# Measured times in a list schedule, and operand copies moved to GpSimd

## The chip, the cores and the metric

The kernel runs on one core of a Trainium2 chip. The metric is the device time of one execution in microseconds (us); the runs shown are summed up by their median. TensorE (PE in the profile; PEld is its weight load) multiplies matrices, ScalarE (ACT), VectorE (DVE) and GpSimd (POOL) work on elements, and SyncE (SP) issues most of the DMAs.

## What is computed

Two layers over 256 tokens of width 1024, all in float32. Each layer is a SwiGLU block of hidden width 2816, a token mixer, and a second SwiGLU block, with an RMSNorm ahead of and behind each:

```python
for layer in range(DEPTH):                       # DEPTH = 2
    x = x + 0.5 * rmsnorm(swiglu(rmsnorm(x, g[0]), ...), g[1])
    x = x + rmsnorm(token_mixer(rmsnorm(x, g[2]), w_in, w_out, ...), g[3])
    x = x + 0.5 * rmsnorm(swiglu(rmsnorm(x, g[4]), ...), g[5])
```

The mixer projects to queries, keys and values and runs 16 heads of three kinds side by side: 6 dilated softmax heads ("dil"), 4 differential heads ("diff", the difference of two softmaxes, with queries and keys of width 32) and 6 stick-breaking heads ("stick"). Their outputs are joined and multiplied by `w_out`.

## The kernel before, in words

Each float32 operand of a large product is split into a high part that TensorE multiplies at full speed (type fp32r) and the rest, and a product is three matmuls: high by high, high by low, low by high (`mm3`; every matmul is issued in `mm`, line 403). A weight tile of 128 x 1024 is loaded into one of 5 "raw" buffers, ScalarE writes its high part (line 306) and VectorE the rest (line 309) into one of 10 "ring" buffers.

The program is not written in its running order. `op(engine, us, fn, after, bufs)` notes each step with an estimate of its time. `Program.run` then plays the program through: TensorE's steps get due times in the order in which they were noted, the steps of the other engines get theirs backward from the steps that need them, and whenever an engine is free in this play the most urgent step is issued whose inputs are ready and whose buffers are free. That fixes the order of instructions on each engine. On the chip each engine goes through its list in that order and waits where an input is late. The estimates come from `act_us(n, psum)` and `dve_us(n)` (lines 240 to 245) or stand as figures at the `op`. A hop between engines counts as 0.2 us.

In `mixer` the eight pairs of heads (two heads of one kind, or for diff two heads with two scores each) are taken in the order diff, stick, dil, stick, diff, stick, dil, dil. `qk(i)` projects queries and keys of pair i: two weight tiles, 24 matmuls each, into a PSUM tile. Then operands for the scores are made from it:

- diff (lines 782 to 800): each of the four 32-row blocks gets a tile of its own in which the high part stands twice and the low part twice. ScalarE writes both high copies (line 790, two instructions), VectorE the low part (794) and its copy (795).
- stick and dil (lines 802 to 820): one of the two operands, the "moving" one, is needed with both halves of the partitions exchanged as well. ScalarE writes each half twice (line 806, four instructions; two for the other operand), VectorE the low parts (810), and GpSimd copies the low parts of the moving operand into the other half (814).

`pair(i)` then computes the scores (`scores`, lines 839 to 868: matmuls, VectorE's `least` at 859, ScalarE's `expo` at 863), normalises, transposes, and multiplies with the values; for stick it runs the softplus chain (940 to 951). `stage` interleaves qk(i) with the steps of pairs i-1 and i-2. The products with `w_out` (`out_`, 6 matmuls for a step) and the residual of the first 128 tokens, and then those of the second, close the mixer.

Of the kernel before, what the change touches and what calls it, by code (L numbers as in the profile page):

```python
# [8 lines left out]
F32 = mybir.dt.float32  # L9
F32R = mybir.dt.float32r  # L10
BF16 = mybir.dt.bfloat16
AF = mybir.ActivationFunctionType
# [112 lines left out]
class Program:  # L125
# [7 lines left out]
    def op(self, eng, dur, fn, after=(), bufs=(), spare=None, lag=None):  # L133
        o = Op()
        o.eng, o.dur, o.fn, o.after, o.bufs = eng, dur, fn, [a for a in after if a is not None], list(bufs)
        o.spare, o.lag, o.idx = spare or {}, lag, len(self.ops)
        for b in o.bufs:
            b.left += 1
        self.ops.append(o)
        return o  # L140
# [97 lines left out]


def act_us(n, psum, extra=0):  # L240
    return (0.05 if psum else 0.092) + 0.000833 * n + 0.093 * extra


def dve_us(n):
    return 0.068 + 0.00104 * n


def trunk(tc, x, norm_gains, w_gate, w_up, w_down, w_in, w_out, dlam, subln, consts, out):
    nc = tc.nc
# [6 lines left out]
    op = G.op  # L256
# [16 lines left out]
    QB = tuple(slice(32 * m, 32 * (m + 1)) for m in range(4))  # L273
    HB = (slice(0, 64), slice(64, 128))
# [464 lines left out]
    def mixer(l, xt, turn1, g, nxt, o_cst, o_misc):  # L739
# [17 lines left out]
        tab = [None]  # L757
        qk_, mixed, stages = {}, {}, []

        def qk(i):  # L760

            kind, n = PAIRS[i]
            sc = {"dil": -0.125, "stick": 0.125, "diff": -(32 ** -0.5)}[kind]
            moving = 0 if kind == "stick" else 1
            r = {}
            for part in range(2):  # L770
                h = half_chunk(wi, QK_OFF[kind][part] + 128 * n)
                p = Buf(PS)
                scale = sc if part == 0 else 1.0

                o = None
                for ks in steps(STEPS_Q):
                    def pe(h=h, p=p, ks=ks):
                        w = [t.rearrange("p (k c) -> p k c", k=8) for t in h.ring.t]
                        for k in ks:
                            mm3(p.t[:, :256], w[0][:, k, :], w[1][:, k, :], xt.hi(k, slice(0, 256)), xt.lo(k, slice(0, 256)), k == 0, k == KC - 1)  # L780

                    o = op("PE", 0.327 * len(ks), pe, [o] + sum(xt.done, []) + h.ready, [p, xt.b, h.ring])
                if kind == "diff":
                    for m in range(4):
                        b = Buf(QS, F32R)
                        two = m ^ (2 if part == 0 else 1)

                        def fhi(p=p, b=b, m=m, two=two, scale=scale):
                            for e in (m, two):
                                nc.scalar.activation(b.t[QB[e], :], p.t[QB[m], :256], AF.Copy, scale=scale)  # L790

                        def flo(p=p, b=b, m=m, two=two, scale=scale):
                            e, f = [e for e in range(4) if e not in (m, two)]
                            nc.vector.scalar_tensor_tensor(b.t[QB[e], :], p.t[QB[m], :256], scale, b.t[QB[m], :].bitcast(F32), OP.mult, OP.subtract)  # L794
                            nc.vector.tensor_copy(b.t[QB[f], :], b.t[QB[e], :].bitcast(F32))  # L795

                        o1 = op("ACT", act_us(256, True) * 2, fhi, [o], [p, b])
                        r[part, m] = (b, op("DVE", dve_us(256) + 0.2, flo, [o1], [p, b]))
                    continue
                bs = [Buf(QS, F32R) for _ in range(2)]  # L800
                lo = bs if part != moving else [Buf(QS, F32R) for _ in range(2)]

                def fhi(p=p, bs=bs, scale=scale, both=part == moving):
                    for b in range(2):
                        for e in range(2 if both else 1):
                            nc.scalar.activation(bs[b].t[HB[b ^ e], :], p.t[HB[b], :256], AF.Copy, scale=scale)  # L806

                def flo(p=p, bs=bs, lo=lo, scale=scale, other=part != moving):
                    for b in range(2):
                        nc.vector.scalar_tensor_tensor(lo[b].t[HB[b ^ other], :], p.t[HB[b], :256], scale, bs[b].t[HB[b], :].bitcast(F32), OP.mult, OP.subtract)  # L810

                def fcopy(lo=lo):
                    for b in range(2):
                        nc.gpsimd.tensor_copy(lo[b].t[HB[b ^ 1], :], lo[b].t[HB[b], :].bitcast(F32))

                o1 = op("ACT", act_us(256, True) * (4 if part == moving else 2), fhi, [o], [p] + bs)
                o2 = op("DVE", dve_us(256) * 2, flo, [o1], [p] + bs + (lo if part == moving else []))
                if part == moving:
                    o2 = op("POOL", 0.9, fcopy, [o2], lo)
                r["m" if part == moving else "s"] = bs  # L820
                if part == moving:
                    r["l"] = lo
                r.setdefault("o", []).extend([o1, o2])
            qk_[i] = r
# [13 lines left out]
        def scores(i, r0, n, h, den, d0):  # L838

            qk = qk_[i]  # L840
            p, sn, mn, e = Buf(PS), Buf(SN), Buf(SM), Buf(ES)
            o = C_BIAS + 256 * h
            if n == 32:
                (q, oq), (k, ok) = qk[0, r0 // 32], qk[1, r0 // 32]
                bufs, after, us = [q, k], [oq, ok], 0.22

                def pe():
                    mm(p.t[:, 0:256], q.t[:, B], k.t, True)
                    mm(p.t[:, 256:384], q.t[:, A], k.t[:, A], False, True)
            else:  # L850
                b = r0 // 64
                bufs, after, us = [qk["s"][b], qk["m"][b], qk["l"][b]], qk["o"], 0.40

                def pe():
                    products(p, i, b, ((SEG[0], B, slice(0, 256)), (SEG[1], A, A)))

            def least():
                for a, bs in ((0, slice(o, o + 256)), (1, slice(o + 128, o + 256))):
                    nc.vector.tensor_tensor_reduce(sn.t[:, SEG[a]], p.t[:, SEG[a]], cst[:, bs], 1.0, 3.0e38, OP.add, OP.min, mn.t[:, a:a + 1])  # L859

            def expo():
                for a in range(2):
                    nc.scalar.activation(e.t[:, SEG[a]], sn.t[:, SEG[a]], AF.Exp, bias=mn.t[:, a:a + 1], scale=-1.0, accum_out=den.t[:, d0 + a:d0 + a + 1])  # L863

            o1 = op("PE", us, pe, after, bufs + [p], spare={PS: 2})
            o2 = op("DVE", 0.56, least, [o1, o_cst], [p, sn, mn])
            o3 = op("ACT", 0.88, expo, [o2, tab[0]], [sn, mn, e, den])
            return e, o3

        def transposed(e, oe, c_eng):  # L870
# [18 lines left out]
        def pair(i):  # L889

            kind, n = PAIRS[i]
            c = CHUNK0[kind] + n
            pt = [None, None]
            if kind == "dil":
                es = []
                for b in range(2):
                    den, r = Buf(SM), Buf(SM)
                    e, o = scores(i, 64 * b, 64, 2 * n + b, den, 0)

                    def norm(e=e, den=den, r=r):  # L900
                        nc.vector.reciprocal(r.t[:, 0:2], den.t[:, 0:2])
                        for a, s in enumerate(SEG):
                            nc.vector.tensor_scalar(e.t[:, s], e.t[:, s], r.t[:, a:a + 1], None, OP.mult)

                    es.append((e, op("DVE", 0.67, norm, [o], [e, den, r])))
                yield
                for b in range(2):
                    pt[b] = transposed(*es[b], b)
# [1 line left out]
            elif kind == "diff":  # L910
                es = []
                for b in range(2):
                    den, r = Buf(SM), Buf(SM)
                    (e1, o1), (e2, o2) = (scores(i, 64 * b + 32 * a, 32, N_DIL + 2 * n + b, den, 2 * a) for a in range(2))

                    def comb(e1=e1, e2=e2, den=den, r=r):
                        nc.vector.reciprocal(r.t, den.t)
                        nc.vector.tensor_scalar(r.t[:, 2:4], r.t[:, 2:4], nlam[:, l:l + 1], None, OP.mult)
                        for a, s in enumerate(SEG):
                            nc.vector.tensor_scalar(e2.t[:, s], e2.t[:, s], r.t[:, 2 + a:3 + a], None, OP.mult)  # L920
                        for a, s in enumerate(SEG):
                            nc.vector.scalar_tensor_tensor(e1.t[:, s], e1.t[:, s], r.t[:, a:a + 1], e2.t[:, s], OP.mult, OP.subtract)

                    es.append((e1, op("DVE", 1.6, comb, [o1, o2] + o_misc, [e1, e2, den, r])))
                yield
                for b in range(2):
                    pt[b] = transposed(*es[b], b)
# [1 line left out]
            else:  # L929
                qk = qk_[i]  # L930
                zs = []
                for b in range(2):
# [14 lines left out]
                    def fhi(az=az, sh=sh):  # L947
                        nc.scalar.activation(sh.t[:, :384], az.t, AF.Copy)
# [24 lines left out]
            p = Buf(PS)  # L973
# [201 lines left out]
```

## Time and profile before

| what | us |
|---|---|
| median of 3 runs | 991.08 (990.92 to 991.38) |
| the profiled execution | 991.41 |
| its span, first to last instruction | 989.6 |
| TensorE busy in it | 973.5 |
| VectorE busy | 634.3 |
| ScalarE busy | 595.4 |
| GpSimd busy | 29.5 |

A view by stretches gives for each stretch how long each engine was busy, how many instructions started, and the clock granted to TensorE (1.00 is 2.4 GHz, 0.50 is 1.2 GHz). A view of waits gives for an engine and line what the instruction waited for. A timeline gives instructions in order of time, neighbours of one kind merged (x24), with the idle time before in brackets. "L403" is line 403 of the kernel before.

### The profile page before, as it was taken

The page shows a single profiled execution, that of the slowest core. Times are in us where ns is not written, and L with a number is a line of the kernel's source. Part 1 is how long each engine was busy: PE and PEld are TensorE (multiplying, and loading weights), DVE is VectorE, ACT ScalarE, POOL GpSimd, SP SyncE. Part 2 cuts the span into 40 slices and gives each one's busy share as a digit, 9 for nine tenths or more (in the row PEclk, how much of TensorE's full clock was granted, in tenths as well). Part 3 has the DMA queues.
Part 4 walks back from the last instruction along what each step waited for, and adds up shares of the span by engine and source line. Part 5 has one row for each costly group of instructions (what it writes and reads, how often), then busy time and mean ns, then how long its engine had stood idle before and what let it go on. Part 6 is the DMA issues. An engine that isn't in the chain of part 4 may idle for free.

```text
span 989.6 us, 17271 instructions
## 1 busy us (share of the span) xinstructions
PE 973.5 (98%) x6664; PEld 883.9 (89%) x6664; DVE 634.3 (64%) x1161; ACT 595.4 (60%) x1205; POOL 29.5 (3%) x62
## 2 busy tenths in 40 slices
PE   8999999999999999999999999999999999999997
PEld 6999999888988899999889999998888889999996
DVE  6765544778898656455686555459698876646433
ACT  7754444769997555444665444347899776444442
POOL 0000000000000000000010000001010000000000
PEclk9999999999999999999999999999999999999999
DMA  8986664684336766664577666557732557666531
GB/s 270 325 282 198 189 181 144 200 242 114 126 91 207 255 193 189 197 188 149 173 226 241 194 191 193 169 153 238 213 102 84 167 174 240 189 197 189 165 107 42
DMA packets 147316, 182.79 MB, mean 185 GB/s; under 512 B 6177, under 2 KB 125217, under 8 KB 147106
## 3 DMA queue, kind: packets, MB, share of 16 engines
q1 hardware_dynamic: 147090, 181.43, 59.7%
q8 instruction: 52, 0.85, 0.3%
q10 hardware_dynamic: 144, 0.26, 0.1%
q14 instruction: 30, 0.25, 0.1%
HBM read 180.62 MB, written 1.05 MB: 184 GB/s over the span
## 4 chain that ended last, share of the span: by engine, by line
PE 89%; ACT 6%; DVE 3%; issue 1%; DMA 1%; DVEq 0%; SPq 0%; ACTq 0%
PE ps L403 87%; ACT q L790 2%; ACT ring L306 1%; PE ps L537 1%; DVE q L794 1%; ACT e L863 1%; ACT q L806 1%; DMA raw<-in_w_in 1%; DVE q L795 0%; DVE sn L859 0%; PE ps L637 0%; DMA grow<-in_norm_gains 0%; DVE ring L309 0%; PE ps L874 0%; ACT junk L446 0%
## 5 line engine op out<-in xcount | busy, mean ns | idle before, releaser
L306 ACT ACTIVATE ring<-raw 128x512 fp32r<-128x512 f32 (+1 forms) x596 | 372.4, 667 | 308.9 <-issue 207.0
L309 DVE TENSOR_TENSOR ring<-raw,ring 128x512 fp32r<-128x512 f32 (+1 forms) x596 | 417.7, 740 | 182.9 <-ACT ring L306 177.9
L403 PE MATMUL ps<-xt,ring 128*128 128x256 f32 x4320 | 507.1, 278 | 0.0
L403 PEld LDWEIGHTS ps<-xt,ring 128*128 128x128 f32 x4320 | 501.6, 188 | 5.5 <-issue 1.7
L403 PE MATMUL ps<-ring,h 128*128 128x512 f32 x1248 | 298.2, 393 | 0.0
L403 PEld LDWEIGHTS ps<-ring,h 128*128 128x128 f32 x1248 | 229.7, 188 | 47.4 <-issue 0.7
L403 PE MATMUL ps<-ring,xt 128*128 128x512 f32 (+1 forms) x576 | 124.4, 373 | 0.1
L403 PEld LDWEIGHTS ps<-ring,xt 128*128 128x128 f32 x576 | 101.0, 188 | 19.3 <-DVE xt L543 0.3
L669 DVE TENSOR_TENSOR e<-ps,e 128x512 f32<-128x512 f32 x37 | 25.6, 692 | 111.7 <-PE ps L403 111.7
L670 ACT ACTIVATE h<-e 128x512 fp32r<-128x512 f32 x37 | 23.4, 633 | 22.4 <-DVE e L669 22.0
L482 DVE TENSOR_TENSOR e<-ps,gpo 128x512 f32<-128x512 f32 x24 | 16.3, 688 | 20.6 <-ACT junk L446 20.2
L446 ACT ACTIVATE junk<-ps 128x512 bf16<-128x512 f32 x24 | 14.2, 593 | 23.9 <-PE ps L403 23.7
L806 ACT ACTIVATE q<-ps 64x256 fp32r<-64x256 f32 x72 | 27.2, 377 | 1.0
L666 ACT ACTIVATE e<-ps 128x512 f32<-128x512 f32 x37 | 21.9, 593 | 5.8 <-PE ps L403 5.8
L671 DVE TENSOR_TENSOR h<-e,h 128x512 fp32r<-128x512 f32 x37 | 25.3, 684 | 0.0
L863 ACT ACTIVATE e<-sn,sm 128x256 f32<-128x256 f32 (+1 forms) x56 | 24.7, 446 | 0.1
L790 ACT ACTIVATE q<-ps 32x256 fp32r<-32x256 f32 x64 | 24.0, 375 | 0.9
L456 POOL TENSOR_SCALAR sm<-sm 128x1 f32<-128x1 f32 x13 | 7.7, 594 | 538.4 <-ACT junk L446 538.4
L403 PE MATMUL ps<-q,q 128*128 128x256 f32 (+1 forms) x128 | 20.5, 283 | 2.8 <-DVE q L795 2.8
L403 PEld LDWEIGHTS ps<-q,q 128*128 128x128 f32 x128 | 18.1, 191 | 4.6 <-issue 2.3
L810 DVE SCALAR_TENSOR_TENSOR q<-ps,q 64x256 fp32r<-64x256 f32 x48 | 20.2, 421 | 1.2
L540 ACT ACTIVATE xt<-ps 128x512 fp32r<-128x512 f32 x24 | 13.1, 590 | 11.5 <-PE ps L537 11.4
(93 smaller groups left out, 407.4 us busy)
## 6 DMA issues: line engine op xcount, KB each, us to landing
raw<-in_w_ffn_gate SPq DMA_DIRECT2D x88, 512.0 KB, 4.8
raw<-in_w_ffn_up SPq DMA_DIRECT2D x88, 512.0 KB, 4.6
raw<-in_w_ffn_down SPq DMA_DIRECT2D x88, 512.0 KB, 4.4
raw<-in_w_in SPq DMA_DIRECT2D x32, 512.0 KB, 5.9
raw<-in_w_out SPq DMA_DIRECT2D x16, 512.0 KB, 4.0
raw<-in_w_in SPq DMA_DIRECT2D x16, 384.0 KB, 4.3
gpo<-in_norm_gains SPq DMA_DIRECT2D x6, 512.0 KB, 5.6
gpr<-in_norm_gains SPq DMA_DIRECT2D x5, 512.0 KB, 6.2
```

The lines of the kernel that those rows point to most:

```text
L306: nc.scalar.activation(h.at(0, s), raw.t[:, s], AF.Copy)
L309: nc.vector.tensor_tensor(h.at(1, s), raw.t[:, s], h.at(0, s).bitcast(F32), OP.subtract)
L403: nc.tensor.matmul(o, a, b, start=start, stop=stop, skip_group_check=True)
L482: nc.vector.tensor_tensor(y.t, accs[i].t, gv(), OP.mult)
L666: a = op("ACT", act_us(512, True), lambda p=p: nc.scalar.activation(sg.t, p.t, AF.Silu), os[-1:] + hold, [p, sg])
L669: m_ = op("DVE", dve_us(512), lambda p=p: nc.vector.tensor_tensor(sg.t, p.t, sg.t, OP.mult), os[-1:] + [a], [p, sg])
L670: o1 = op("ACT", act_us(512, False), lambda: nc.scalar.activation(bh.t, sg.t, AF.Copy), [m_], [sg, bh])
L671: o2 = op("DVE", dve_us(512), lambda: nc.vector.tensor_tensor(bl.t, sg.t, bh.t.bitcast(F32), OP.subtract), [o1], [sg, bh, bl])
L790: nc.scalar.activation(b.t[QB[e], :], p.t[QB[m], :256], AF.Copy, scale=scale)
L806: nc.scalar.activation(bs[b].t[HB[b ^ e], :], p.t[HB[b], :256], AF.Copy, scale=scale)
L810: nc.vector.scalar_tensor_tensor(lo[b].t[HB[b ^ other], :], p.t[HB[b], :256], scale, bs[b].t[HB[b], :].bitcast(F32), OP.mult, OP.subtract)
L863: nc.scalar.activation(e.t[:, SEG[a]], sn.t[:, SEG[a]], AF.Exp, bias=mn.t[:, a:a + 1], scale=-1.0, accum_out=den.t[:, d0 + a:d0 + a + 1])
```

## The change

The estimates of ScalarE's and VectorE's steps grow in the list schedule: `act_us`, `dve_us` and five figures at the scores. The second copies move to GpSimd: for diff the copy of the low part goes from VectorE (line 795) to a step of its own on GpSimd; for the moving operand of stick and dil the second copy of the high part goes from ScalarE (two of the four instructions of line 806) to GpSimd, beside the copy of the low part that GpSimd makes already. The scores' matmuls wait for these copies.

```diff
 def act_us(n, psum, extra=0):
-    return (0.05 if psum else 0.092) + 0.000833 * n + 0.093 * extra
+    return (0.11 if psum else 0.15) + 0.00087 * n + 0.19 * extra
 
 
 def dve_us(n):
-    return 0.068 + 0.00104 * n
+    return 0.13 + 0.001 * n
...
                         def flo(p=p, b=b, m=m, two=two, scale=scale):
                             e, f = [e for e in range(4) if e not in (m, two)]
                             nc.vector.scalar_tensor_tensor(b.t[QB[e], :], p.t[QB[m], :256], scale, b.t[QB[m], :].bitcast(F32), OP.mult, OP.subtract)
-                            nc.vector.tensor_copy(b.t[QB[f], :], b.t[QB[e], :].bitcast(F32))
+
+                        def fcopy(b=b, m=m, two=two):
+                            e, f = [e for e in range(4) if e not in (m, two)]
+                            nc.gpsimd.tensor_copy(b.t[QB[f], :], b.t[QB[e], :].bitcast(F32))
 
                         o1 = op("ACT", act_us(256, True) * 2, fhi, [o], [p, b])
-                        r[part, m] = (b, op("DVE", dve_us(256) + 0.2, flo, [o1], [p, b]))
+                        o2 = op("DVE", dve_us(256), flo, [o1], [p, b])
+                        r[part, m] = (b, op("POOL", 0.47, fcopy, [o2], [b]))
                     continue
...
-                def fhi(p=p, bs=bs, scale=scale, both=part == moving):
+                def fhi(p=p, bs=bs, scale=scale):
                     for b in range(2):
-                        for e in range(2 if both else 1):
-                            nc.scalar.activation(bs[b].t[HB[b ^ e], :], p.t[HB[b], :256], AF.Copy, scale=scale)
+                        nc.scalar.activation(bs[b].t[HB[b], :], p.t[HB[b], :256], AF.Copy, scale=scale)
...
-                def fcopy(lo=lo):
+                def fcopy(ts):
                     for b in range(2):
-                        nc.gpsimd.tensor_copy(lo[b].t[HB[b ^ 1], :], lo[b].t[HB[b], :].bitcast(F32))
-
-                o1 = op("ACT", act_us(256, True) * (4 if part == moving else 2), fhi, [o], [p] + bs)
+                        nc.gpsimd.tensor_copy(ts[b].t[HB[b ^ 1], :], ts[b].t[HB[b], :].bitcast(F32))
+
+                o1 = op("ACT", act_us(256, True) * 2, fhi, [o], [p] + bs)
                 o2 = op("DVE", dve_us(256) * 2, flo, [o1], [p] + bs + (lo if part == moving else []))
                 if part == moving:
-                    o2 = op("POOL", 0.9, fcopy, [o2], lo)
+                    o1 = op("POOL", 0.95, lambda bs=bs, fcopy=fcopy: fcopy(bs), [o1], bs)
+                    o2 = op("POOL", 0.95, lambda lo=lo, fcopy=fcopy: fcopy(lo), [o2], lo)
...
-            o2 = op("DVE", 0.56, least, [o1, o_cst], [p, sn, mn])
-            o3 = op("ACT", 0.88, expo, [o2, tab[0]], [sn, mn, e, den])
+            o2 = op("DVE", 0.8, least, [o1, o_cst], [p, sn, mn])
+            o3 = op("ACT", 1.0, expo, [o2, tab[0]], [sn, mn, e, den])
...
-                    es.append((e, op("DVE", 0.67, norm, [o], [e, den, r])))
+                    es.append((e, op("DVE", 0.78, norm, [o], [e, den, r])))
...
-                    es.append((e1, op("DVE", 1.6, comb, [o1, o2] + o_misc, [e1, e2, den, r])))
+                    es.append((e1, op("DVE", 1.8, comb, [o1, o2] + o_misc, [e1, e2, den, r])))
```

## Rows read from the trace of the kernel before

**Rows 1.** By stretches: length, busy us of PE, PEld, DVE, ACT, POOL, then PEclk

```profile
0.00:30.00 30.00, 26.74 (x167) 20.86 (x168) 19.12 (x31) 20.91 (x41) 1.82 (x11) 1.00 0.89 285
30.00:222.00 192.00, 192.00 (x1326) 177.00 (x1325) 116.94 (x183) 105.71 (x183) 6.45 (x11) 1.00 0.70 216
222.00:292.00 70.00, 66.68 (x536) 62.32 (x534) 62.45 (x181) 68.07 (x180) 5.68 (x12) 0.98 0.40 118
292.00:707.00 415.00, 415.00 (x2740) 375.68 (x2739) 253.80 (x397) 224.65 (x417) 9.87 (x16) 1.00 0.64 196
707.00:777.00 70.00, 66.36 (x539) 61.47 (x538) 62.42 (x180) 68.15 (x180) 5.69 (x12) 1.00 0.41 119
777.00:980.00 203.00, 203.00 (x1353) 183.96 (x1353) 116.91 (x189) 105.75 (x202) 0.00 (x0) 1.00 0.55 169
980.00:989.60 9.60, 3.69 (x16) 2.66 (x15) 2.71 (x4) 2.17 (x7) 0.00 (x0) 0.89 0.14 55
```

**Rows 2.** Waits of PE: us in total, times, longest

```profile
PE ps L403 <- DVE q L795: 2.8, 8, 0.5
PE ps L874 <- DVE e L922: 2.0, 3, 0.9
PE ps L403 <- DVE e L951: 1.9, 2, 1.0
```

**Rows 3.** Timeline, first diff pair of layer 0: start, us, what

```profile
229.71 0.41 DVE L794 SCALAR_TENSOR_TENSOR q<-ps,q 32x256 fp32r<-32x256 f32 x1
230.59 0.41 PE L403 MATMUL ps<-q,q 128*128 128x256 f32 x2 [0.48 <-DVE q L795]
```

**Rows 4.** Groups by line and shape, 230.2 to 290 us, PE: busy, mean ns

```profile
L403 PE MATMUL ps<-xt,ring 128*128 128x256 f32 x288 | 38.2, 290 | 0.0
```

**Rows 5.** By stretches, line 309 alone (VectorE): length, busy us (instructions), PEclk

```profile
230.20:255.20 25.00, 6.69 (x10) 0.93 0.32 95
```

**Rows 6.** By stretches, line 403 alone: length, PE and PEld busy, PEclk

```profile
233.15:240.45 7.30, 7.30 (x52) 7.30 (x51) 0.77 0.12 21
...
718.88:724.60 5.72, 5.72 (x53) 5.72 (x53) 1.00 0.00 2
```

**Rows 7.** Groups by line and shape, whole span: busy us, mean ns, idle before

```profile
L806 ACT ACTIVATE q<-ps 64x256 fp32r<-64x256 f32 x72 | 27.2, 377 | 1.0
...
L790 ACT ACTIVATE q<-ps 32x256 fp32r<-32x256 f32 x64 | 24.0, 375 | 0.9
...
L810 DVE SCALAR_TENSOR_TENSOR q<-ps,q 64x256 fp32r<-64x256 f32 x48 | 20.2, 421 | 1.2
...
L794 DVE SCALAR_TENSOR_TENSOR q<-ps,q 32x256 fp32r<-32x256 f32 x32 | 13.4, 419 | 9.0 <-ACT q L790 8.3
...
L814 POOL CAST q<-q 64x256 fp32r<-64x256 f32 x24 | 11.4, 474 | 161.3 <-DVE q L810 160.4
...
L795 DVE CAST q<-q 32x256 fp32r<-32x256 f32 x32 | 9.1, 285 | 1.1
```

**Rows 8.** Timeline around the wait at 268 us

```profile
265.60 0.42 DVE L794 SCALAR_TENSOR_TENSOR q<-ps,q 32x256 fp32r<-32x256 f32 x1 [1.13 <-ACT q L790]
...
268.49 1.19 PE L403 MATMUL ps<-e,trir 128*128 128x384 f32 x7 [0.86 <-DVE e L951]
```

**Rows 9.** Timeline, close of the mixer of layer 0

```profile
302.23 11.18 PE L403 MATMUL ps<-ring,h 128*128 128x512 f32 x48
...
311.31 1.42 DVE L508 SCALAR_TENSOR_TENSOR pt<-xs,sm,gpr 128x512 f32<-128x512 f32 x2 [0.51 <-ACT sm L466]
...
313.24 1.03 PE L537 MATMUL ps<-cst,pt 128*128 128x128 f32 x8
```

**Rows 10.** Timeline, GpSimd beside VectorE's line 309

```profile
197.32 0.30 POOL L456 TENSOR_SCALAR sm<-sm 128x1 f32<-128x1 f32 x1 [6.92 <-ACT junk L446]
...
199.84 2.49 DVE L309 TENSOR_TENSOR ring<-raw,ring 128x512 fp32r<-128x512 f32 x4
...
200.93 1.57 POOL L456 TENSOR_SCALAR sm<-sm 128x1 f32<-128x1 f32 x1 [2.67 <-ACT junk L446]
```

**Rows 11.** GpSimd's line 814: durations min/median/max in ns

```profile
L814 POOL CAST q<-q x24: 393/399/854, 233.3 to 774.9; 64x256 fp32r<-64x256 f32 x24
```

## The prediction

> **What bounds the kernel now.** I read the view by stretches first [rows 1]. TensorE is busy 973.5 of 989.6 us, and what matters is where the other 16.1 us lie. The SwiGLU blocks show none: 192.00 of 192.00, 415.00 of 415.00, 203.00 of 203.00. The first 30 us lack 3.3 us and the last 9.6 us lack 5.9 us; the change touches nothing there but order. The rest is in two stretches of 70 us, one for each mixer: 70 - 66.68 = 3.32 us and 70 - 66.36 = 3.64 us, 6.96 us in all. The reader is to see what the other engines do in just these stretches: ScalarE is busy 68.1 of 70 and VectorE 62.4, while over the whole span they stand near 60%. So the kernel is bound by TensorE, except in the mixers, where three engines are nearly full at once and TensorE waits.
>
> The view of TensorE's waits says for what [rows 2]: eight waits for a diff operand (line 795, 2.8 us), three for the combined differential weights (922, 2.0 us) and two for the stick chain (951, 1.9 us). All end on VectorE, and 6.7 of the 6.96 us are accounted for.
>
> Two more facts decide what can be had. First, TensorE had other work. After 230.2 us in layer 0 it still ran 288 of the projection matmuls, which is 12 weight tiles of 24 [rows 4], while VectorE prepared only 10 more halves of such tiles, 5 tiles [rows 5]. So at the first wait about 7 prepared tiles lay in the ring, some 20 us of work at 5.7 us for two [rows 6], and TensorE stood in front of scores whose operands were late [rows 3]. That is a fault of the order, and the order comes from the estimates. Second, the clock: 48 projection matmuls follow the first waits in both mixers. In layer 0 their stretch was granted 0.77, so a part of it ran at the 1.2 GHz level, and lasted 7.30 us; in layer 1 it kept 1.00 and lasted 5.72 us with one instruction more [rows 6]. So the idle time before it (1.5 us in layer 0, 1.3 in layer 1) costs 1.6 us more in one of the two.
>
> The prize is thus 6.96 + 1.6 = 8.6 us, and no more, since everything else on TensorE is dense and its matmuls are unchanged.
>
> **The change part by part.**
>
> Copies off ScalarE. Line 806 has 72 instructions of 377 ns [rows 7], 36 in a mixer; 6 pairs lose two each, 12 x 0.377 = 4.5 us of ScalarE for a mixer, out of 68.1 busy in 70.
>
> Copies off VectorE. Line 795 has 32 of 285 ns [rows 7], 16 in a mixer: 4.6 us of VectorE for a mixer, out of 62.4. They lie where they hurt: the scores of a diff pair come at the pace of 0.419 + 0.285 us and a gap per operand, and the wait of 0.86 us at 268 us is for line 951, which stands in VectorE's queue behind three such operands [rows 8]. Three copies less are 0.86 us, just that wait.
>
> Copies onto GpSimd. They cost 40 casts for a mixer instead of 12. A cast of line 814 takes 399 ns when alone and 854 at most [rows 11], mean 474 [rows 7]; 28 more are 13 us in a stretch of 70 where GpSimd is busy 5.7 [rows 1]. It has room; what counts is the delay. For stick and dil the moving operand had four ScalarE copies, two VectorE steps and two casts in a row, 4 x 0.377 + 2 x 0.421 + 2 x 0.40 = 3.15 us; now two ScalarE copies, then GpSimd's two casts beside VectorE's two steps, then two casts: 0.75 + 0.84 + 0.80 = 2.4 us, 0.75 us sooner, if no cast is held. For diff a last cast of 0.40 to 0.85 us takes the place of 0.285 us, and a hop to another engine is added: the first operand comes 0.1 to 0.6 us later and the fourth about as much earlier, since VectorE's pace falls from 0.77 to 0.42 us and GpSimd's is 0.40 at best. No 32-row cast on GpSimd is in the trace; the 64-row cast is the nearest row, and I take 0.40 to 0.85 with 0.47, its mean. Behind a waiting cast stand only other operand casts: in the mixers GpSimd has nothing else.
>
> Who is held? The trace shows a price for GpSimd beside VectorE: an instruction of line 456 that takes 0.30 us took 1.57 when it met four instructions of line 309 back to back, and ended only after them [rows 10]. The Trainium skill states this as a rule ("SBUF — State Buffer", section "Who interferes with whom"): a VectorE instruction with two SBUF inputs and a GpSimd instruction that reads SBUF shut each other out for a whole instruction. Line 309 is such an instruction, so the rule speaks against the change, and the trace agrees with it by the 1.57 us. By the measured mean the loss is small: 24 casts took 11.4 us, 1.8 us above 24 x 0.40 [rows 7, 11], 3 us for 40 casts, on an engine with 50 us free. It becomes a rival below.
>
> The estimates. For 256 columns out of PSUM `act_us` gave 0.263 us and now gives 0.333, against 0.375 to 0.377 measured; `dve_us` 0.334, now 0.386, against 0.42 [rows 7]. A diff operand was planned at 0.53 us on each of ScalarE and VectorE and took 0.75 and 0.77. So the old plan had scores ready earlier than they were and put them ahead of the ready projections; with the new figures it should fill the gap from the seven tiles. The five figures at the scores grow too. In the SwiGLU blocks estimates only move due times; TensorE has no gap there and VectorE and ScalarE are busy about 0.6 of the time [rows 1], which hides it. I take nothing, with 0.5 us either way for the first 30 us, where they are busier.
>
> What is late next? If TensorE gains 4.9 us by 280 us in layer 0, the end of the mixer comes earlier only if ScalarE and VectorE finish the last pairs earlier too. ScalarE loses 4.5 us of work, VectorE 4.6: about what is needed. The cover at the close is thin: the 36 or so matmuls with w_out behind the first residual run until 313.24, when the transposes start, and their input (line 508) is done at 312.73 [rows 9]. Only 0.5 us is spare.
>
> The sum. 991.4 for the profiled execution, less 8.6 if every wait goes. I keep one wait of about 0.95 us for each mixer, the size of those at 268 us [rows 8], because two of the three kinds hang on chains that the new order only moves, and 0.9 us for one step of w_out drawn out of the cover (1.4 us a step, 11.18 / 8 [rows 9], less the spare 0.5): 2 x 0.95 + 0.9 = 2.8. So 991.4 - 8.6 + 2.8 = 985.6; the median lies 0.33 below the profiled execution: 985.3.
>
> **The rivals.**
>
> A wait for a wait: the freed time is spent elsewhere. The waits on lines 922 and 951 come back on other pairs, the clock falls once as now, and only 2 us or less is won: 989.1 to 993. For it: two engines stay over 85% full in the stretch (68.1 - 4.5 and 62.4 - 4.6 of 70). Against it: the seven ready tiles.
>
> Slower, by the cover. With scores planned at 0.8 and 1.0 us, the plan sees TensorE idle near the end of the pairs and draws steps of w_out for the second 128 tokens ahead of the first residual's close. Each then leaves that close bare: the first costs 0.9 us, each further one 1.4. At three or fewer in each mixer (3.7 us x 2 = 7.4) the gain of 8.6 still pays; at five (6.5 x 2 = 13.0) the time is 991.1 - 8.6 + 13.0 = 995.5. It decides from about four on.
>
> Slower, by held casts, without a better order. If each cast of the first diff pair is held to 0.854 us, the four scores come 0.3 to 0.7 us later than now, the first two waits grow to over 2 us, and the clock falls in layer 1 as well (1.6 us): 991.1 + 2 x 0.7 + 1.6 = 994.1. The trace bears it out in some casts only (0.854 at most, 0.399 at the median [rows 11]), so I give it little. This is the rule of the Trainium skill named above ("SBUF — State Buffer", "Who interferes with whom") at its full price.
>
> **How the numbers follow.** Forecast 985.3 with its own range of 982.2 to 989: 0.68. Wait for a wait: 0.18. Slower by the cover: 0.08. Slower by held casts: 0.06. A measurement of this kernel can tell some 0.2%, 2 us, from no change: faster 0.68, same 0.18, slower 0.14. The low end is the floor, 991.1 - 8.6 = 982.5, with 0.3 for the start. The upper end takes in the second case whole and part of the slower ones: 993.6.
>
> **What would show it.** Right: in the stretches of 70 us TensorE idle falls from 3.3 and 3.6 to about 1 each, ScalarE's busy time falls by 4.5 us and VectorE's by 4.6 for each mixer, projection matmuls stand ahead of the first diff scores, and the clock stays at 1.00 in layer 0. Casts of 0.40 to 0.85 us on GpSimd, 80 in all, with TensorE seldom waiting for them. Wrong: idle time at the transposes behind the first residual (the cover), TensorE waiting for GpSimd in front of diff scores (held casts), or idle time in the SwiGLU blocks, which I priced at nothing.

## The result: 1.1% slower

The changed kernel takes 1002.29 us (median of 3 runs, 1002.23 to 1003.01) against 991.08: a ratio of 1.0113, 95% interval 1.010 to 1.0127. The profiled execution has a span of 1000.5 us, against 989.6 before.

By stretches, in the columns of [rows 1], the changed kernel shows both what was forecast and what was not:

```profile
222.00:292.00 70.00, 69.07 (x545) 64.03 (x544) 59.30 (x161) 65.36 (x167) 18.35 (x40) 1.00 0.41 120
292.00:320.00 28.00, 21.25 (x115) 16.48 (x114) 24.83 (x56) 21.64 (x59) 0.00 (x0) 0.90 0.67 211
...
707.00:787.00 80.00, 78.93 (x608) 72.63 (x606) 67.81 (x181) 73.68 (x185) 18.77 (x40) 1.00 0.46 135
787.00:812.00 25.00, 18.07 (x97) 13.89 (x92) 21.68 (x43) 18.45 (x50) 0.00 (x0) 0.88 0.68 217
```

The first and third rows answer to the two mixer rows of [rows 1]. TensorE's idle time inside the mixers is nearly gone: 0.93 us where there were 3.32, and 1.07 in a stretch of 80 us where there were 3.64 in 70; the clock stays at 1.00 in layer 0. The second and fourth rows are the closes of the mixers, where TensorE had no gap before. Now it idles 6.75 and 6.93 us there, and the granted clock of the two stretches is 0.90 and 0.88. A part of that fall lies in the idle time itself, where it costs nothing. What it costs is to be read behind the long waits, from TensorE's rows alone (length, busy, PEclk):

```profile
317.71:322.00 4.29, 4.29 (x16) 0.60 0.62 211
...
809.12:814.00 4.88, 4.88 (x18) 0.64 0.57 192
```

That is 4.29 x 0.40 = 1.7 and 4.88 x 0.36 = 1.8 us of full clock lost while TensorE worked. TensorE's waits name the place (us in total, times, longest):

```profile
PE ps L537 <- DVE pt L508: 12.9, 3, 6.4
...
PE ps L403 <- DVE pt L885: 1.3, 2, 0.7
PE ps L403 <- ACT h L889: 1.0, 2, 0.5
```

The waits of [rows 2] are off the list. In their place stands one line, the transposes behind the first residual (537), waiting for the normed rows (508). The timeline of layer 0's close, to be laid beside [rows 9]:

```profile
301.02 4.38 PE L403 MATMUL ps<-ring,h 128*128 128x512 f32 x18
...
302.90 0.55 DVE L907 TENSOR_SCALAR e<-e,sm 128x256 f32<-128x256 f32 x2
...
305.24 0.27 PE L878 MATMUL ps<-cst,e 128*128 128x128 f32 x1
...
308.40 3.04 PE L403 MATMUL ps<-ring,h 128*128 128x512 f32 x12 [0.48 <-ACT h L889]
...
316.81 1.41 DVE L508 SCALAR_TENSOR_TENSOR pt<-xs,sm,gpr 128x512 f32<-128x512 f32 x2 [0.21 <-ACT sm L466]
317.71 1.94 PE L537 MATMUL ps<-cst,pt 128*128 128x128 f32 x8 [6.27 <-DVE pt L508]
```

Two things are to be seen. Before, nine steps of w_out ran behind the last pair: 48 matmuls in front of the transposes [rows 9], and the last step behind them:

```profile
314.03 1.63 PE L403 MATMUL ps<-ring,h 128*128 128x512 f32 x6
```

By the order of the program the 48 are three steps that finish the first 128 tokens and five of the second (pairs 2 to 6), and these five, 30 matmuls, are what covered the residual. In the changed kernel 12 matmuls stand behind the last pair: the last step of each half, the only two that need this pair. So all five were run earlier, the last step now stands in front of the transposes, and TensorE runs out of work at 311.4 and waits 6.27 us for the residual's chain. And the steps were run in the way of the pairs: the last pair's normalised weights are ready at 303.45 (line 907), but their transposes (878) start only at 305.24, because 18 w_out matmuls stand ahead of them in TensorE's queue.

### The profile page after: what moved, and what is told of

The parts are those of the page before. It is cut to its first block, busy times and chain, and to the rows that moved or that the text cites. A ratio compares the mean times of both kernels' runs of the same rounds, so it can differ in the third digit from the quotient of the medians.

```text
span 1000.5 us, 17303 instructions
## 1 busy us (share of the span) xinstructions
PE 976.0 (98%) x6664; PEld 884.6 (88%) x6664; DVE 628.5 (63%) x1129; ACT 589.8 (59%) x1181; POOL 59.2 (6%) x118
## 4 chain that ended last, share of the span: by engine, by line
PE 91%; ACT 4%; DMA 3%; DVE 1%; issue 1%; POOL 0%; DVEq 0%; SPq 0%; POOLq 0%; ACTq 0%
PE ps L403 89%; PE ps L537 1%; ACT q L790 1%; DMA raw<-in_w_ffn_down 1%; ACT junk L446 1%; DMA raw<-in_w_ffn_up 1%; DMA raw<-in_w_ffn_gate 1%; ACT ring L306 1%; DMA grow<-in_norm_gains 0%; PE ps L637 0%; ACT q L809 0%; DVE ring L309 0%; DVE q L794 0%; DVE pt L508 0%; POOL q L798 0%
## 5 line engine op out<-in xcount | busy, mean ns | idle before, releaser
L403 PE MATMUL ps<-ring,h 128*128 128x512 f32 x1248 | 301.7, 394 | 1.6 <-ACT h L889 1.0
L403 PE MATMUL ps<-ring,xt 128*128 128x512 f32 (+1 forms) x576 | 127.9, 380 | 0.0
L537 PE MATMUL ps<-cst,pt 128*128 128x128 f32 x96 | 16.3, 312 | 13.0 <-DVE pt L508 12.9
L537 PEld LDWEIGHTS ps<-cst,pt 128*128 128x128 f32 x96 | 13.3, 162 | 17.0 <-issue 14.9
L817 POOL CAST q<-q 64x256 fp32r<-64x256 f32 x48 | 23.8, 495 | 42.6 <-ACT q L809 18.2
L794 DVE SCALAR_TENSOR_TENSOR q<-ps,q 32x256 fp32r<-32x256 f32 x32 | 13.4, 420 | 14.1 <-ACT q L790 13.4
```

Of the source, the lines that this page charges most:

```text
L403: nc.tensor.matmul(o, a, b, start=start, stop=stop, skip_group_check=True)
L537: nc.tensor.transpose(p.t[:, 128 * k:128 * (k + 1)], h.t[:, 128 * k:128 * (k + 1)], ident)
L817: nc.gpsimd.tensor_copy(ts[b].t[HB[b ^ 1], :], ts[b].t[HB[b], :].bitcast(F32))
```

## The experiments

The theory (A): the new estimates make the planner draw the w_out steps of the second 128 tokens ahead, which bares the first residual and delays the pairs; the copies help. The rival (B): the copies on GpSimd make the pairs late, and the close with them. Each kernel was timed beside the kernel before; ratios are to that.

### The two halves of the change

`copies_only` is the changed kernel with every old estimate:

```diff
-    return (0.11 if psum else 0.15) + 0.00087 * n + 0.19 * extra
+    return (0.05 if psum else 0.092) + 0.000833 * n + 0.093 * extra
-    return 0.13 + 0.001 * n
+    return 0.068 + 0.00104 * n
...   (and 0.56, 0.88, 0.67, 1.6 at scores, norm and comb)
```

> The copies on GpSimd as in the change, every estimate of ScalarE and VectorE as before. Theory A (the new estimates draw the w_out products ahead of the first residual, the copies themselves help): the close of the mixers keeps its cover, idle there under 1 us each, and the waits on lines 795, 922 and 951 shrink; 984 to 989 us. Theory B (the copies on GpSimd make the pairs late and so the close): idle at the close of 4 us or more in each mixer; 997 us or more.

Measured: 991.42 us, ratio 1.0003 (0.9993 to 1.0012). Neither number fits. The close keeps its cover, so B falls, but the relief brings nothing measurable. Its mixers by stretches:

```profile
222.00:292.00 70.00, 67.32 (x539) 62.15 (x538) 61.06 (x171) 67.42 (x174) 19.62 (x40) 1.00 0.42 127
707.00:777.00 70.00, 67.27 (x530) 62.16 (x529) 60.36 (x165) 66.34 (x172) 19.48 (x40) 0.98 0.41 122
```

TensorE's idle time falls only from 3.32 to 2.68 and from 3.64 to 2.73 us, and ScalarE is still busy 67.4 and 66.3 us of 70: with the old order the freed time was filled and TensorE still waited.

`estimates_only` is the kernel before with the new functions and figures, and no copy moved.

> All new estimates, the copies where they were before. Theory A: 5 to 7 us idle at the transposes behind the first residual in each mixer and a fall of the clock there; 999 to 1006 us (the copies' relief is missing too). Theory B: no idle at the close; 988 to 993 us.

Measured: 1004.73 us, ratio 1.0139 (1.0124 to 1.0155), with waits of 5.3 and 5.5 us at the transposes. The estimates alone make the loss. By the medians it is larger than with the copies, but the two intervals just touch. A stands.

### The cover given back

`after_cover` is the changed kernel with one more input for the w_out steps that were drawn ahead. No other line is changed, but the program is played through anew, so steps of the close on ScalarE and VectorE move along:

```diff
-        def out_(i, T, ns):
+        def out_(i, T, ns, late=()):
...
-            o = op("PE", 0.65 * len(ns), pe, [om] + done[2 * T] + done[2 * T + 1] + h.ready, ...
+            o = op("PE", 0.65 * len(ns), pe, [om] + done[2 * T] + done[2 * T + 1] + h.ready + list(late), ...
...
         for i in range(2, n - 1):
-            out_(i, 1, (0, 1))
+            out_(i, 1, (0, 1), done[0] + done[1])
```

> The changed kernel, but the w_out steps of the second 128 tokens for pairs 2 to 6 are noted as waiting for the last step of the first 128 tokens, so that none of them can be drawn ahead. Theory A: the cover of the first residual comes back, idle at the close under 1 us each, and the inner gain of the mixers stays: 983 to 989 us. Theory B (the pairs end late for another reason): TensorE then waits for the pairs instead, idle of 4 us or more between 280 and 310 us; 996 us or more.

Measured: 987.25 us, ratio 0.9963 (0.9949 to 0.9977): 15.0 us under the changed kernel and 3.6 under the one before. Its stretches of layer 0, and its timeline at the close:

```profile
222.00:292.00 70.00, 69.07 (x544) 63.99 (x543) 59.36 (x161) 65.79 (x168) 18.33 (x40) 1.00 0.39 117
...
292.00:322.00 30.00, 28.94 (x154) 22.73 (x154) 26.72 (x58) 24.41 (x66) 0.00 (x0) 1.00 0.60 191
```

```profile
301.32 9.84 PE L403 MATMUL ps<-ring,h 128*128 128x512 f32 x42
310.99 0.60 PE L537 MATMUL ps<-cst,pt 128*128 128x128 f32 x4
```

The inner stretch is as dense as in the changed kernel, and 42 matmuls stand in front of the transposes, which start without a wait. The last pair ends sooner too, though none of its steps was changed:

| kernel | last product with the values ends, layer 0 (us) | ratio |
|---|---|---|
| before | 302.3 | 1 |
| changed | 307.9 | 1.0113 |
| after_cover | 301.4 | 0.9963 |
| before_bare (below) | 302.0 | 1.0176 |
| estimates_cover (below) | 309.7 | 1.0080 |

With the w_out steps held back, the last pair ends 6.5 us sooner than in the changed kernel: its lateness there came from steps that stood ahead of it, and not from the copies.

### The order at the close alone

`before_bare` is the kernel before with nothing but these steps noted earlier:

```diff
         for i in range(3, n - 1):
             out_(i, 0, (0, 1))
+            out_(i - 1, 1, (0, 1))
+        out_(n - 2, 1, (0, 1))
         out_(n - 1, 0, (0,))
...
-        for i in range(2, n - 1):
-            out_(i, 1, (0, 1))
```

> The kernel before, all estimates and copies as they were; only the w_out steps of the second 128 tokens for pairs 2 to 6 are noted ahead of the last step of the first 128 tokens, so that they run there. If the order at the close alone makes the loss: the first residual starts some 7 us later, TensorE idles 4 to 7 us at the transposes behind it in each mixer, 999 to 1006 us. If it needs pairs made late by copies or estimates: idle at the close under 2 us, 990 to 994 us.

Measured: 1008.76 us, ratio 1.0176 (1.0163 to 1.0189), somewhat over the range of A. Estimates and copies are the old ones and the pairs end on time, yet TensorE waits at the same line:

```profile
301.93 12.53 PE L403 MATMUL ps<-ring,h 128*128 128x512 f32 x54
320.43 1.94 PE L537 MATMUL ps<-cst,pt 128*128 128x128 f32 x8 [5.96 <-DVE pt L508]
```

All 54 remaining matmuls run first, the residual starts behind them, and nothing is left to cover it. An order at the close is worth 17 us in this kernel.

### Do the estimates gain without the copies?

`estimates_cover` is estimates_only with the cover kept as in after_cover.

> All new estimates, the copies where they were before, and the cover kept as in after_cover. If the copies on GpSimd are what fills the inner waits of the mixers: 990 to 993 us, idle inside the mixers near 3 us each. If the new order alone fills them: 986 to 988.5 us.

Measured: 998.75 us, ratio 1.0080 (1.0067 to 1.0093). The copies are needed, and more than was expected. With the cover kept, the new order costs 0.8% without the copies and wins 0.4% with them; the copies with the old order win nothing. The timeline of this kernel shows the pairs 7 us late:

```profile
308.15 1.57 PE L403 MATMUL ps<-pt,h 128*64 128x256 f32 x8
310.20 8.46 PE L403 MATMUL ps<-ring,h 128*128 128x512 f32 x36 [0.47 <-ACT h L885]
```

To see which engine's relief matters, after_cover was run with only one kind of copy on GpSimd. `diff_copies_cover` takes the moving operand's high copies back to ScalarE (line 806 as before), `moving_copies_cover` takes the diff copies back to VectorE (lines 794 and 795 as before).

> after_cover with only the diff copies on GpSimd (VectorE is relieved by 4.6 us a mixer); the second copies of the moving operand's high part are back on ScalarE. If ScalarE is what holds the pairs: 994 us or more, near estimates_cover (998.75). If VectorE is: 987 to 990 us.

> after_cover with only the moving operand's copies on GpSimd (ScalarE is relieved by 4.5 us a mixer); the diff copies are back on VectorE. If ScalarE is what holds the pairs: 986 to 990 us. If VectorE is: 994 us or more.

Measured: 995.94 us, ratio 1.0047 (1.0032 to 1.0062), and 993.37 us, ratio 1.0027 (1.0018 to 1.0036). By the ratios, from 1.0080 without copies, relieving VectorE wins 0.33%, ScalarE 0.53% and both 1.17%. Neither expectation held: it takes both, and together they are worth 0.31%, some 3 us, more than the sum. That excess, and the lead of ScalarE's relief over VectorE's, are hardly larger than the intervals, and the order on TensorE changes with each kernel, so these shares are not clean.

### Which estimates

The change has four new figures beside the two functions, not five as said above. `after_old_scores` is the changed kernel with the old figures 0.56, 0.88, 0.67 and 1.6 at the scores, norm and comb; `after_old_funcs` the changed kernel with the two old functions and the new figures.

> The changed kernel with the four figures at the scores, the normalising and the combination back at 0.56, 0.88, 0.67 and 1.6 us; the functions for ScalarE and VectorE stay new. If those figures alone draw the w_out products ahead: idle at the close under 1.5 us each, 984 to 990 us. If the two functions are enough to do it: 998 us or more.

> The changed kernel with the two functions back at the old figures; the figures at scores, normalising and combination stay new. With the functions new and the figures old 997.2 us were measured, so the functions make about half of the loss. If the two parts add: 994 to 998 us and some 3 us idle at each close. If one needs the other (the planner draws steps ahead only when it sees both engines late): idle at the close under 1 us, 985 to 990 us.

Measured: 997.15 us, ratio 1.0067 (1.0052 to 1.0082), with 3.5 and 3.4 us idle at the closes; and 1001.19 us, ratio 1.0101 (1.0088 to 1.0114), with 3.2 and 3.4 us. Either part is enough to draw steps ahead; the two losses, 6.3 and 9.8 us over the kernel before, add to more than the 11.2 of both. In after_old_funcs the wait is at another place:

```profile
PE ps L403 <- ACT xt L540: 5.7, 2, 2.9
```

Here the transposes are still covered, but the one w_out step that stood behind them, while ScalarE took their result out of PSUM (line 540), was drawn ahead.

Both were run with the cover kept as well: `old_scores_cover` and `old_funcs_cover`.

> The changed kernel with the figures at scores, normalising and combination back at the old ones, and the cover kept. The figures were too large by the pace at which these steps follow each other in the trace (0.56, 0.88 and 1.6 us were the measured pace). If their error still costs inside the mixers once the cover is kept: faster than after_cover (987.25), 984 to 986.5 us. If the cover was all that they cost: 987 to 989 us.

> The changed kernel with the two functions old, the figures at the scores new, and the cover kept. Without the cover it took 1001.2 us, 3 us of TensorE's wait in each mixer being for ScalarE behind the transposes, where the step of w_out that stood there before was drawn ahead. If that step comes back with the cover: 988 to 992 us.

Measured: 986.68 us, ratio 0.9953 (0.9941 to 0.9965), and 988.02 us, ratio 0.9972 (0.9962 to 0.9983). With the cover kept, all three sets of new estimates win 0.3 to 0.5%, and their intervals overlap: what the estimates are exactly matters little, what they did to the close mattered. The first is the fastest version measured; it beats both kernels, as after_cover does.

### Are the casts on GpSimd beside other work?

`casts_twice` is after_cover with each operand cast written twice:

```diff
+                            for _ in range(2):
-                            nc.gpsimd.tensor_copy(b.t[QB[f], :], b.t[QB[e], :].bitcast(F32))
+                                nc.gpsimd.tensor_copy(b.t[QB[f], :], b.t[QB[e], :].bitcast(F32))
...   (and the same in the other fcopy)
```

> after_cover with every operand cast on GpSimd written twice, so that each takes some 0.4 us more and GpSimd's queue is twice as long; the plan and the order are unchanged. If the casts on GpSimd lie beside other work: 987 to 988.5 us and TensorE's waits for GpSimd under 1 us. If the scores hang on them (held casts): 992 us or more, with TensorE waiting for GpSimd in front of the scores.

Measured: 994.41 us, ratio 1.0031 (1.002 to 1.0041), 7.2 us over after_cover. Its first wait and GpSimd's two groups:

```profile
PE ps L403 <- POOL q L799: 4.2, 6, 0.9
```

```profile
L819 POOL CAST q<-q 64x256 fp32r<-64x256 f32 x96 | 53.3, 555 | 30.4 <-ACT q L810 23.6
...
L799 POOL CAST q<-q 32x256 fp32r<-32x256 f32 x64 | 27.8, 438 | 66.1 <-DVE q L794 62.8
```

So the scores do hang on the casts: they have little slack, though GpSimd is busy only 18.3 of 70 us in after_cover. The casts do not cost by way of a slower VectorE: it is busy 628.5 us over the span, against 627.4 in after_cover. With the casts once, TensorE's matmuls wait 0.2 us for them in after_cover, and in the changed kernel no such wait is listed. At their real length they fit, and at twice their length they don't.

## Why the prediction was wrong

**What bounds the kernel.** Right: three engines nearly full in the mixers, and TensorE waiting for VectorE in front of ready projections. With the cover kept, the new order and the copies together do remove most of the inner waits.

**The prize.** Oversized. Of the 8.6 us, 1.6 were for the fall of the clock in layer 0. The kernel before shows that it cost next to nothing: from the first diff score to the stick matmuls behind line 951 layer 0 took 268.49 - 230.59 = 37.90 us [rows 3, 8], and layer 1, which kept its clock, as long:

```profile
716.33 0.42 PE L403 MATMUL ps<-q,q 128*128 128x256 f32 x2 [0.21 <-DVE q L795]
...
754.17 1.18 PE L403 MATMUL ps<-e,trir 128*128 128x384 f32 x7 [1.04 <-DVE e L951]
```

754.17 - 716.33 = 37.84 us. Both stretches end on a wait for VectorE's line 951, of 0.86 and 1.04 us: VectorE's chain came last there, and the slower matmuls lay beside it. I priced the two stretches of [rows 6] by themselves, without asking what ends last behind them. Without the 1.6 the floor is 991.1 - 6.96 = 984.1; the fastest version measured is 986.68.

**The estimates.** The step that failed. The prediction said that the new figures would fill the gap "from the seven tiles", and priced the close at "0.9 us for one step of w_out drawn out of the cover", in one of the mixers. The planner knows no difference between projections and w_out steps: it takes whatever is ready. Five steps went ahead in each mixer, not one in one of them. The prediction's own price for five, 0.9 + 4 x 1.4 = 6.5 us a mixer, is what the closes show as idle time, 6.75 and 6.93 us: the rival had the mechanism that came and, as one of its cases, the right number of steps. It was given 0.08, without a count of the steps that the plan would find ready. Its figure of 995.5 still fell 6.8 short. It kept the whole gain of 8.6, where the mixers' idle time fell by 4.96, and had no fall of the clock in it, which cost 3.5 at the two closes.

**What is late next.** Half right. The cover was named as thin, 0.5 us, and it was what broke (it was 30 matmuls, not "36 or so"). The reason given for hope was wrong: the pairs were to end earlier because ScalarE and VectorE lose 4.5 us each. They ended 5.6 us later, behind the drawn steps, and only 0.9 us earlier with the cover kept.

**The copies.** The instructions that left had taken 9.1 us on ScalarE and 9.1 on VectorE over both mixers, as forecast (2 x 4.5 and 2 x 4.6). The sign that was named, a fall of the engines' busy time by as much, did not come in full: over the span ScalarE's fell from 595.4 to 589.8 us and VectorE's from 634.3 to 628.5, some 2.9 a mixer. Why the rest of their busy time grew is not shown. GpSimd's casts came out as bounded:

```profile
L817 POOL CAST q<-q 64x256 fp32r<-64x256 f32 x48 | 23.8, 495 | 42.6 <-ACT q L809 18.2 <-PE ps L403 13.6 <-DVE q L813 8.7
L798 POOL CAST q<-q 32x256 fp32r<-32x256 f32 x32 | 13.3, 419 | 74.2 <-DVE q L794 72.7
```

80 casts in 37.1 us, where 80 x 0.474 = 38 were taken. That the copies win by themselves was wrong: copies_only is level with before. That the rival of held casts gets little was right for this change, but "an engine with 50 us free" was no reason: in casts_twice the second cast of each cost 7.2 us on an engine that is busy little more than half of the mixers.

**The SwiGLU blocks.** Priced at nothing, with no gap expected. The changed kernel idles 0.45 us between 320 and 707 us and 0.01 between 812 and 990; that held.

**What stays open.** Why the new estimates cost 0.8% without the copies even when the cover is kept. The pairs end 7 us later there, and no single wait in the profile accounts for it. Of the 7.6 us that the span grew by, 2.5 are idle time of TensorE; for the other 5.1 it is busy longer, 978.6 against 973.5 us for as many matmuls. The granted clock was 0.91 from 222 to 240 us and 0.79 from 292 to 300, so a part of this is time at the 1.2 GHz level. What in the new order brings it about was not tested.

## What to carry to other kernels

In a list schedule the ready work that hides one gap may be the cover of another: before a better estimate is put in, ask which steps it will draw forward, and what they stand in front of now. An order that must hold (here, that the second half's steps follow the first half's close) belongs in the schedule as a dependency and should not be left to the estimates; one added input turned 1.1% slower into 0.4% faster. And the price of a slow stretch is what ends later behind it, not its own length.

## What the runs showed of the hardware

A GpSimd cast of 256 columns takes as long for 32 partitions as for 64: the median is 395 ns for line 798 and 397 for line 817 of the changed kernel. And VectorE was seen to be held beside GpSimd as well. Line 951 of the kernel before, with two inputs in SBUF, is line 955 after (durations min/median/max in ns):

```profile
L951 DVE TENSOR_TENSOR e<-sn,e x12: 549/552/559, 246.9 to 771.3; 128x384 fp32r<-128x384 f32 x12
```

```profile
L955 DVE TENSOR_TENSOR e<-sn,e x12: 551/559/776, 243.4 to 781.7; 128x384 fp32r<-128x384 f32 x12
```

With 80 casts on GpSimd instead of 24 its longest took 776 ns, where before none took over 559. In layer 0 two casts and two of these instructions began together, and each took longer than alone (casts 399 ns at the median before, [rows 11]):

```profile
243.36 1.07 POOL L817 CAST q<-q 64x256 fp32r<-64x256 f32 x2 [2.11 <-ACT q L809]
243.39 1.45 DVE L955 TENSOR_TENSOR e<-sn,e 128x384 fp32r<-128x384 f32 x2
```

This agrees with the Trainium skill ("SBUF — State Buffer", section "Who interferes with whom"), by which either side of such a pair may be the one held.
